# Half of the query projection moved into the pair products of a hybrid encoder layer

## The chip, the cores and the metric

The kernel runs on one core of one Trainium2 chip. The metric is device time in microseconds of one launch. Before the change it is 678.65 us, the median of three runs (678.29 to 679.68). The core has a matmul engine (TensorE, PE in the profile; its weight loads are PEld), a vector engine (VectorE, DVE), a scalar engine (ScalarE, ACT), a general engine (GpSimd, POOL) and a queue that issues the transfers (SyncE, SP). Each takes its own instructions strictly in order and waits for the others by semaphores.

## What is computed

One layer over 1024 tokens of width 1024, in float32: a layer norm, one input projection whose columns are cut into eight parts, two branches, and an output projection with a second layer norm.

```
proj = layer_norm(x) @ w_in                    # 1024 x 5120
q, k, v, z_a, u, z_b, g_a, g_b = split(proj)   # 4 x 512, 2 x 512, 2 x 1024
attn = neighbourhood_attention(q, k, v, rpb)   # 8 heads of 64, q scaled by 1/8
u = centred_depthwise_conv(u, conv_w, conv_b)
h = rg_lru(u, forward) + rg_lru(u, reverse)    # decay exp(-8 softplus(-lam) * gate)
m = sigmoid(g_a + b) * ((attn * silu(z_a)) @ w_ba) + sigmoid(g_b + b) * ((h * silu(z_b)) @ w_bb)
out = layer_norm(alpha * x + m @ w_out)
```

## The kernel before

**Numbers as high and low parts.** A matmul operand is kept as two tiles: a rounded "high" part (a cast, `..._hi`) and the "low" remainder (a subtraction, `lo_of`, line 128). A product of two such operands is three matmuls (`mm3`, line 134): high by high, high by low, low by high.

**First stage: layer norm, v and half of q.** The tokens are eight tiles of 128. `tile_in(i)` transposes tile i on TensorE into four blocks of the activation: B11, B21 hold the first four tiles, B12, B22 the last four; the first index is the half of the 1024 features. `v_part` and `q_part` multiply those blocks with weights directly. q is 512 columns, in four blocks m of 128; each `q_part(m, n)` with n for the half of the tokens is 24 matmuls of 512 columns. Before, all four m are made in this way: m = 0, 1 for the first tokens between the v parts, and six parts, (0, 1), (1, 1), (2, 0), (2, 1), (3, 0), (3, 1), behind the last v part. Each part is emptied by ScalarE (`q_hi`, scaled by 1/8) and VectorE (`q_lo`) and stored to `q_d`.

**The pairs.** The rest of `w_in`, except v, is done in pairs of 128-column blocks: 16 pairs. Each pair is a 2 x 2 block product in Winograd's form, with 7 block products in place of 8, in the order `OPS` = a11, a12, s2, s1, s3, s4, a22. A product is one slot, 4 x 3 = 12 matmuls of 512 columns. The loop over `7 * N_PAIR + 4` slots (line 1003) is the backbone of the middle of the kernel. The weights' side needs sums s1 to s4 of the pair's four blocks (`s_sum`, VectorE) and each operand's high (`s_hi`, ScalarE, or GpSimd for those in `HI_POOL` from pair 1 on) and low (`s_lo`, VectorE, or GpSimd for a11 and a22). The activations' side needs B11, B21, B22 and four sums T1 to T4, made once per tile 4 to 7:

- `t_full(i)`: t1, t2, t3 of the tile, one copy on ScalarE and four steps on VectorE;
- `t_last(i)`: t4 from t2 and B21, two steps on VectorE (lines 309 and 310);
- `t_hi`, `t_lo`: high on ScalarE, low on GpSimd.

Only a22, the last product of a pair, uses T4. The products s2, s3 and a22 add into the PSUM bank of a11 and s4 into that of s1. Between two of them `evacuate` copies the bank out on ScalarE (tiles u1 to u3, lines 939 to 945) or adds it on VectorE, so the next product into the bank waits for that.

**What a pair's result becomes** is set by the list `takes`: `take_u` for the convolution input, `take_zg` for gates, `take_k` for keys. A consumer may return two later steps, run one and two slots after.

**Slots.** Convolution, gates of the recurrence and the loads for the next stages are put at fixed slots (`CONV_AT`, `GATE_AT`, `LATE_AT`, `HEAD_AT`). Weights of pair p + 2 are loaded in the fifth slot of pair p (`s_load`). Pairs listed in `U_PAIRS` take no extra PSUM bank.

**The change of stage.** Behind the last q part the first stage's pools are released and PSUM is split anew into six banks for the pairs and two for the gates. There the decay rates of the recurrence (softplus of lam by a series, lines 626 to 642: one ScalarE exponential and some thirty tiny VectorE steps) are worked out, all in one block ahead of pair 0's VectorE work.

The order on ScalarE, VectorE, GpSimd and the SP queue is the order in which the code is written; TensorE's too. Attention, the branch projections, the merge and the output projection follow the pairs and aren't touched.

Of the kernel before, what the change touches and what calls it, by code (L numbers as in the profile page):

```python
# [10 lines left out]
F32 = mybir.dt.float32  # L11
# [28 lines left out]
BLOCKS = (1, 0, 6, 2, 3, 4, 5, 7)  # L40
# [27 lines left out]
def encoder_kernel(ctx, tc, x, gb1, gb, w_qk, w_v, w_s, w_ba, w_bb, w_gate, smalls, bias, w_out, out):  # L68
# [58 lines left out]
    def lo_of(eng, lo, full, hi):  # L127
        eng.tensor_tensor(lo, full, hi.bitcast(F32), ALU.subtract)  # L128
# [160 lines left out]
    def f(t, i):  # L289
        return t[:, :, ti(i)].bitcast(F32)  # L290

    def t_full(i):

        tt[i, 3] = wsp.tile([P, 4, P], F32, tag="a22", bufs=2, name=f"t3_{i}")[:]
        t12 = ln.tile([P, 2, 4, P], F32, tag="x", bufs=5, name=f"t12_{i}")
        tt[i, 1], tt[i, 2] = t12[:, 0], t12[:, 1]
        if i in (4, 6):
            tt["last"] = ln.tile([P, 2, 4, P], F32, tag="x", bufs=5, name=f"t4_{i}")
        tt[i, 4] = tt["last"][:, i % 2]
        t1, t2, t3 = (tt[i, c] for c in (1, 2, 3))  # L300
        A.copy(t3, tp4(i, 0))
        V.tensor_tensor(t1, tp4(i, 0), f(B11[0], i), ALU.subtract)
        V.tensor_tensor(t1, t1, f(B11[1], i), ALU.subtract)
        V.tensor_tensor(t2, tp4(i, 1), t1, ALU.subtract)
        V.tensor_tensor(t3, tp4(i, 1), t3, ALU.subtract)

    def t_last(i):
        t4 = tt[i, 4]
        V.tensor_tensor(t4, f(B21[0], i), tt[i, 2], ALU.subtract)
        V.tensor_tensor(t4, t4, f(B21[1], i), ALU.add)  # L310

    def t_hi(i, *cs):
        for c in cs:
            A.copy(Ts[c][0][:, :, ti(i)], tt[i, c])
# [54 lines left out]
    def s_load(p, *names):  # L369
        for o in names if p < N_PAIR else ():  # L370
            t = wsp.tile([P, 4, P], F32, tag=o, bufs=2 if o == "a22" else 1, name=f"{o}_{p}f")
            SP.dma_start(t[:], w_s[p, ("a11", "a21", "a12", "a22").index(o)])
            s_a[p, o] = t

    def s_sum(p, *names):
        for o in names if p < N_PAIR else ():
            a, b, op = dict(s1=("a21", "a22", ALU.add), s2=("s1", "a11", ALU.subtract),
                            s3=("a11", "a21", ALU.subtract), s4=("a12", "s2", ALU.subtract))[o]
            t = s_a[p, o] = wsp.tile([P, 4, P], F32, tag=o, name=f"{o}_{p}f")
            V.tensor_tensor(t[:], s_a[p, a][:], s_a[p, b][:], op)  # L380

    def s_hi(p, o):
        if p < N_PAIR:
            s_w[p, o] = pair(wsp, [P, 4, P], f"w{o}_{p}", tag="w" + o)
            (G.tensor_copy if p and o in HI_POOL else A.copy)(s_w[p, o][0][:], s_a[p, o][:])
# [157 lines left out]
    q_part(0, 0, slice(256, HALF))  # L543
    t_last(4)
    tile_in(5)
    q_hi(0, 0)
    t_hi(4, 2, 1, 3, 4)
    t_lo(4, 2, 1, 3, 4)
    tile_lo(5)
    q_lo(0, 0)  # L550
    q_store(0, 0)
    keep(7)
    q_part(1, 0)
    t_full(5)
    q_hi(1, 0)
    q_lo(1, 0)
    q_store(1, 0)
    t_last(5)
    for kind in "hwa":
        v_part(4, kind, KS)  # L560
    tile_in(6)
    v_hi(4)
    t_hi(5, 2, 1, 3, 4)
    t_lo(5, 2, 1, 3, 4)
    tile_lo(6)
    v_lo(4)
    v_store(4)
    t_full(6)
    for kind in "hwa":
        v_part(5, kind, KS)  # L570
    tile_in(7)
    v_hi(5)
    t_hi(6, 2, 1, 3)
    t_lo(6, 2, 1, 3)
    tile_lo(7)
    v_lo(5)
    v_store(5)
    t_last(6)
    t_hi(6, 4)
    t_lo(6, 4)  # L580
# [12 lines left out]
    s_load(0, "a11")  # L593
    for m in range(4):
        for n in BOTH if m > 1 else (1,):
            q_part(m, n)
            if m < 2:
                qk_prep(m + 2)
                if m == 0:
                    qk_load(3)  # L600
                    t_hi(7, 2, 1, 3, 4)
                    t_lo(7, 2, 1, 3, 4)
                    s_load(0, "a21", "a22", "a12")
                else:
                    s_sum(0, "s1", "s2", "s3", "s4")
            q_hi(m, n)
            q_lo(m, n)
            q_store(m, n)
            if m > 1:
                for w in (OPS[:2], OPS[2:4], OPS[4:6], OPS[6:])[2 * (m - 2) + n]:  # L610
                    s_hi(0, w)
                    s_lo(0, w)
    s_load(1, "a11", "a21", "a12", "a22")
    for pl in (ln, wpl, hb12, pst, ps0):
# [10 lines left out]
    lam = sm[:, SM_LAM:SM_LAM + 8]  # L625
    V.tensor_scalar(smh[:], sm[:], 0.5, None, ALU.mult)
    V.tensor_scalar(t0[:], lam, -1.0, None, ALU.mult)
    V.tensor_tensor(t0[:], lam, t0[:], ALU.min)
    A.activation(t0[:], t0[:], AF.Exp)
    V.tensor_scalar(t1[:], t0[:], 2.0, None, ALU.add)  # L630
    V.reciprocal(t1[:], t1[:])
    V.tensor_tensor(t0[:], t0[:], t1[:], ALU.mult)
    V.tensor_tensor(t1[:], t0[:], t0[:], ALU.mult)
    V.tensor_scalar(t2[:], t1[:], 1.0 / 21.0, 1.0 / 19.0, ALU.mult, ALU.add)
    for n in (17, 15, 13, 11, 9, 7, 5, 3, 1):
        V.tensor_tensor(t2[:], t2[:], t1[:], ALU.mult)
        V.tensor_scalar(t2[:], t2[:], 1.0 / n, None, ALU.add)
# [4 lines left out]
    V.tensor_scalar(nsp[:], t0[:], -C_LRU, None, ALU.mult)

# [827 lines left out]
```

## Time and profile before

| what | us |
|---|---|
| median of three runs | 678.65 |
| the profiled execution | 678.46 |
| its span, first to last instruction | 676.7 |
| TensorE busy | 665.2 (98%) |
| VectorE busy | 492.7 (73%) |
| ScalarE busy | 364.5 (54%) |
| GpSimd busy | 355.8 (53%) |

The granted TensorE clock was 0.997 on average. In time, the v parts end near 73 us, the six q parts stand from there to 105.6, the sixteen pairs run to about 426, attention to about 542 and the output to the end.

How the rows read: a row of the timeline gives start, length, engine, line, operation, the tile written and those read, the form and a count; in brackets the idle time before it and what ended it. A row of the chain of waits gives start, length and the work. A row of the waits gives who waited for whom, total, times and longest. "L128" is `lo_of` and "L134" `mm3`, whoever calls them, so the tile names say which step it is. In tile names numbers are left out: `a_0f` is any raw block of pair 0, `s_0f` any sum of it, `wa_h` and `ws_l` its high and low parts, `ht` the T blocks, `t` their full sums.

### The profile page before, as it was taken

The page shows a single profiled execution, that of the slowest core. Times are in us where ns is not written, and L with a number is a line of the kernel's source. Part 1 is how long each engine was busy: PE and PEld are TensorE (multiplying, and loading weights), DVE is VectorE, ACT ScalarE, POOL GpSimd, SP SyncE. Part 2 cuts the span into 40 slices and gives each one's busy share as a digit, 9 for nine tenths or more (in the row PEclk, how much of TensorE's full clock was granted, in tenths as well). Part 3 has the DMA queues.
Part 4 walks back from the last instruction along what each step waited for, and adds up shares of the span by engine and source line. Part 5 has one row for each costly group of instructions (what it writes and reads, how often), then busy time and mean ns, then how long its engine had stood idle before and what let it go on. Part 6 is the DMA issues. An engine that isn't in the chain of part 4 may idle for free.

```text
span 676.7 us, 9344 instructions
## 1 busy us (share of the span) xinstructions
PE 665.2 (98%) x3201; PEld 555.7 (82%) x3201; DVE 492.7 (73%) x821; ACT 364.5 (54%) x612; POOL 355.8 (53%) x258
## 2 busy tenths in 40 slices
PE   8999999999999999999999999999999999999995
PEld 6888888888888887888788888888888878888884
DVE  6978747886998699879967785477787787443434
ACT  6554433256786676669576634477777554210110
POOL 6798632434677576567647444116155456334442
PEclk9999999999999999999999999999999999999998
DMA  8654353233434133431553456998793467412211
GB/s 326 244 179 170 122 206 126 77 110 123 125 128 144 40 103 115 170 126 48 195 178 122 173 191 254 316 366 296 255 323 132 162 220 281 178 62 94 93 63 62
DMA packets 48702, 113.39 MB, mean 168 GB/s; under 512 B 5056, under 2 KB 9744, under 8 KB 47120
## 3 DMA queue, kind: packets, MB, share of 16 engines
q1 hardware_dynamic: 48624, 112.81, 47.2%
q8 instruction: 25, 0.41, 0.3%
q14 instruction: 21, 0.17, 0.1%
q10 hardware_dynamic: 32, 0.01, 0.0%
HBM read 77.11 MB, written 35.68 MB: 167 GB/s over the span
## 4 chain that ended last, share of the span: by engine, by line
PE 89%; DVE 6%; DMA 2%; issue 1%; SPq 1%; ACT 0%; POOL 0%; DVEq 0%; POOLq 0%
PE a L134 30%; PE o L134 13%; PE mb L134 12%; PE s L134 11%; PE q L134 6%; PE v L328 6%; PE acc L1107 3%; PE s L1061 3%; PE pt L1083 3%; PE g L759 2%; DMA wqk_s<-in_w_qk_dram 2%; DVE ws_l L128 1%; PE tp L270 1%; DMA rsb<-rs_d 1%; DVE uc L717 1%
## 5 line engine op out<-in xcount | busy, mean ns | idle before, releaser
L134 PE MATMUL o<-wo_h,ml 128*128 128x512 f32 (+1 forms) x136 | 51.2, 377 | 0.0
L134 PE MATMUL o<-wo_l,mh 128*128 128x512 f32 (+1 forms) x136 | 51.2, 376 | 0.0
L134 PE MATMUL o<-wo_h,mh 128*128 128x512 f32 (+1 forms) x136 | 51.2, 376 | 0.0
L134 PE MATMUL a<-ht_h,ws_h 128*128 128x512 f32 x128 | 50.0, 390 | 0.0
L134 PE MATMUL a<-ht_l,ws_h 128*128 128x512 f32 x128 | 49.8, 389 | 0.0
L134 PE MATMUL a<-ht_h,ws_l 128*128 128x512 f32 x128 | 49.8, 389 | 0.0
L134 PE MATMUL a<-b_h,wa_h 128*128 128x512 f32 x128 | 49.8, 389 | 0.0
L134 PE MATMUL a<-b_h,wa_l 128*128 128x512 f32 x128 | 49.8, 389 | 0.0
L134 PE MATMUL a<-b_l,wa_h 128*128 128x512 f32 x128 | 49.8, 389 | 0.0
L1071 DVE CUSTOM_DVE_ANT_0 sc<-s,bias 128x384 f32<-128x384 f32 (+1 forms) x64 | 33.4, 522 | 21.6 <-PE s L1061 14.2
L1361 DVE SCALAR_TENSOR_TENSOR z<-z,o 128x512 f32<-128x512 f32 (+1 forms) x17 | 11.2, 656 | 51.0 <-PE o L134 51.0
L1091 ACT CAST pt_h<-pt 128x384 fp32r<-128x384 f32 x64 | 29.0, 453 | 25.3 <-PE pt L1083 17.3
L1371 POOL TENSOR_TENSOR z<-z,gb 128x1024 f32<-128x1024 f32 x7 | 16.8, 2400 | 48.5 <-ACT z L1370 48.5
L1076 ACT ACTIVATE p<-sc,summ 128x384 f32<-128x384 f32 (+1 forms) x64 | 37.8, 591 | 5.5 <-DVE summ L1071 5.3
L1340 ACT ACTIVATE sd<-mv,eps_z 128x1 f32<-128x1 f32 x8 | 2.4, 294 | 67.1 <-DVE mv L1366 67.1
L128 DVE TENSOR_TENSOR pt_l<-pt,pt_h 128x384 fp32r<-128x384 f32 x64 | 33.2, 519 | 2.1 <-ACT pt_h L1091 1.6
L328 PE MATMUL v<-wv,b_h 128*128 128x512 f32 x128 | 32.9, 398 | 0.6 <-ACT b_h L279 0.5
L867 POOL CAST wb_h<-wb 128x512 fp32r<-128x512 f32 x9 | 7.0, 779 | 47.4 <-DMA wb<-in_w_bb_dram 47.4
L1061 PE MATMUL s<-ks,qs 128*128 128x384 f32 (+1 forms) x128 | 31.4, 327 | 0.0
L1083 PEld LDWEIGHTS pt<-ident,p 128*128 128x128 f32 x176 | 23.1, 140 | 8.5
L1083 PE MATMUL pt<-ident,p 128*128 128x128 f32 x176 | 29.6, 272 | 0.0
L128 POOL TENSOR_TENSOR wb_l<-wb,wb_h 128x512 fp32r<-128x512 f32 x16 | 22.0, 1375 | 14.3 <-ACT wb_h L865 13.6
(438 smaller groups left out, 2204.2 us busy)
## 6 DMA issues: line engine op xcount, KB each, us to landing
ks<-k_d SPq DMA_DIRECT2D x8, 1024.0 KB, 7.5
h_d<-x SPq DMA_DIRECT2D x8, 512.0 KB, 5.0
v_d<-vs SPq DMA_DIRECT2D x8, 512.0 KB, 3.7
q_d<-q SPq DMA_DIRECT2D x8, 512.0 KB, 3.1
ga_d<-ga SPq DMA_DIRECT2D x16, 256.0 KB, 2.2
gb_d<-gb SPq DMA_DIRECT2D x16, 256.0 KB, 2.6
k_d<-k SPq DMA_DIRECT2D x8, 512.0 KB, 3.4
qs<-q_d SPq DMA_DIRECT2D x8, 512.0 KB, 5.5
```

What stands on the lines that cost most here:

```text
L128: eng.tensor_tensor(lo, full, hi.bitcast(F32), ALU.subtract)
L134: PE.matmul(o, a, b, start=first and i == 0, stop=last and i == len(prods) - 1, skip_group_check=not (first and last))
L328: PE.matmul(vos[i][:], a, wv[kind == "w"][k][:], start=vn[i] == 0, stop=vn[i] == 23)
L759: PE.matmul(o[:, n, :], w[:, 2 * d + b, :], us[b][:, n * HALF:(n + 1) * HALF], start=z == 0, stop=z == 1)
L1061: PE.matmul(o[:, :P * len(near(t))], q[:, t * P:(t + 1) * P], k[:, z, keys], start=z == 0, stop=z == 1)
L1071: V.tensor_tensor_reduce(s[:, :w], o[:, :w], heads[h][2][:, b0:b0 + w], -1.0, 3.0e38, ALU.add, ALU.min, accum_out=sums[h][0][:, t:t + 1])
L1076: A.activation(probs[h % 2][t][:], scs.pop((h, t))[:, :w], AF.Exp, bias=sums[h][0][:, t:t + 1], scale=-1.0, accum_out=sums[h][1][:, t:t + 1])
L1083: PE.transpose(tp[:, n * P:(n + 1) * P], probs[h % 2][t][:, z * P:(z + 1) * P], ident[:])
L1091: A.copy(pt[0][:, span(b)], tps[h, b][:, :P * len(near(b))])
L1107: PE.matmul(acc[g][:, d:d + w], vvs[h // 2][:, b, h % 2, :], pt[:, a:a + w], start=b in (1, 6) and z == 0, stop=z == 1 and b == (4, 7)[g])
L1361: V.scalar_tensor_tensor(z[:, cols], z[:, cols], ALPHA * TWICE, o, ALU.mult, ALU.add)
L1371: G.tensor_tensor(z[:], z[:], gb2[:, 0, :], ALU.mult)
```

## The change

- q's blocks m = 2 and 3 become a new pair 0 (`N_PAIR` 17, first entry 2 in `heads`); the old pairs follow as 1 to 16, and all slot constants move by 7. A new consumer, `take_q`, scales the results by 1/8, splits them and stores them to `q_d`. Of the direct q parts four remain, two of them, (0, 1) and (1, 1), behind the last v part.
- `t_last` of all four tiles moves behind q's last part. t4 takes t2's place, so the tiles for t4 go. The lows of t4 are taken in the order of tiles 7, 4, 5, 6. The full t3 of tiles 5 and 6 lie in other buffers (`a21`, `a12`).
- `t_full(5)` moves ahead of `q_part(1, 0)`, and `t_hi` and `t_lo` stand right behind each `t_full`.
- Pair 0's raw blocks are loaded into other buffers (`ws`, `x`) behind `t_full(6)` and `t_full(7)`; its sums, highs and lows stand between the last v part and the last q part, all highs on ScalarE, all lows on VectorE. Pair 1's blocks are loaded one after the other from `t_full(7)` on.
- The decay rates become a generator, of which one piece is run in each of slots 8 to 13, in pair 1.

```diff
-N_PAIR = 16
+N_PAIR = 17
-CONV_AT = (7, 24, 45, 66)
-GATE_AT = (14, 24, 35, 45, 56, 66, 77, 87)
-LATE_AT = (102, 102, 103, 104, 105)
-HEAD_AT = 109
+CONV_AT = (14, 31, 52, 73)
+GATE_AT = (21, 31, 42, 52, 63, 73, 84, 94)
+LATE_AT = (109, 109, 110, 111, 112)
+HEAD_AT = 116
-U_PAIRS = (0, 5)
+U_PAIRS = (1, 6)
...
-        tt[i, 3] = wsp.tile([P, 4, P], F32, tag="a22", bufs=2, name=f"t3_{i}")[:]
+        tag = ("a22", "a21", "a12", "a22")[i - 4]
+        tt[i, 3] = wsp.tile([P, 4, P], F32, tag=tag, bufs=2 if tag == "a22" else 1, name=f"t3_{i}")[:]
...
     def t_last(i):
-        t4 = tt[i, 4]
-        V.tensor_tensor(t4, f(B21[0], i), tt[i, 2], ALU.subtract)
+        t4 = tt[i, 4] = tt[i, 2]
+        V.tensor_tensor(t4, f(B21[0], i), t4, ALU.subtract)
...
-            lo_of(G if o in LO_POOL else V, lo[:], s_a[p, o][:], hi[:])
+            lo_of(G if p and o in LO_POOL else V, lo[:], s_a[p, o], hi[:])
...
     for kind in "hwa":
         v_part(5, kind, KS)
+    s_load(0, "a11", "a12")
     tile_in(7)
...
     t_full(7)
+    t_hi(7, 2, 1, 3)
+    t_lo(7, 2, 1, 3)
+    s_load(0, "a21", "a22")
+    s_load(1, "a21")
     for kind in "hwa":
         v_part(6, kind, KS)
     v_hi(6)
-    t_last(7)
     v_lo(6)
     v_store(6)
+    s_load(1, "a12")
+    s_sum(0, "s1", "s2", "s3", "s4")
     for kind in "hwa":
         v_part(7, kind, KS)
     v_hi(7)
     v_lo(7)
     v_store(7)
-    s_load(0, "a11")
-    for m in range(4):
-        for n in BOTH if m > 1 else (1,):
-            q_part(m, n)
...
-    s_load(1, "a11", "a21", "a12", "a22")
+    s_load(1, "a11")
+    for o in OPS[:3]:
+        s_hi(0, o)
+        s_lo(0, o)
+    q_part(0, 1)
+    for o in OPS[3:5]:
+        s_hi(0, o)
+        s_lo(0, o)
+    q_hi(0, 1)
+    q_lo(0, 1)
+    q_store(0, 1)
+    s_load(1, "a22")
+    q_part(1, 1)
+    for o in OPS[5:]:
+        s_hi(0, o)
+        s_lo(0, o)
+    t_last(4)
+    q_hi(1, 1)
+    t_hi(4, 4)
+    t_last(5)
+    q_lo(1, 1)
+    q_store(1, 1)
+    for i in (5, 6, 7):
+        if i > 5:
+            t_last(i)
+        t_hi(i, 4)
+    for i in (7, 4, 5, 6):
+        t_lo(i, 4)
...
+    def take_q():
+
+        def consume(mi, n, add, o, c=None):
+            c = o if c is None else c
+            if add is not None:
+                V.tensor_tensor(c[:], add[:], o[:], ALU.add)
+            t = lru.tile([P, 2, HALF], F32R, tag=("us0", "r", "i", "us1")[2 * mi + n], name=f"q2{mi}{n}")
+
+            def high():
+                A.activation(t[:, 0, :], c[:], AF.Copy, scale=0.125)
+
+            def store():
+                V.scalar_tensor_tensor(t[:, 1, :], c[:], 0.125, t[:, 0, :].bitcast(F32), ALU.mult, ALU.subtract)
+                SP.dma_start(q_d[2 + mi][:, :, halves[n]], t[:].bitcast(F32))
+            return [high, store]
+        return consume
...
+    rates = decay_rates()
+    for slot in range(8, 14):
+        at(slot, 1, lambda: next(rates))
...
-    heads = [16, 20, 12, 24, 26, 18, 32, 22, 28, 34, 4, 30, 6, 14, 36, 38]
+    heads = [2, 16, 20, 12, 24, 26, 18, 32, 22, 28, 34, 4, 30, 6, 14, 36, 38]
```

More of the change, by code (lines that the diff above doesn't have):

```diff
@@ L369, in s_load @@
     def s_load(p, *names):
-        for o in names if p < N_PAIR else ():
-            t = wsp.tile([P, 4, P], F32, tag=o, bufs=2 if o == "a22" else 1, name=f"{o}_{p}f")
-            SP.dma_start(t[:], w_s[p, ("a11", "a21", "a12", "a22").index(o)])
+        for z, o in enumerate(names if p < N_PAIR else ()):
+            if p:
+                t = wsp.tile([P, 4, P], F32, tag=o, bufs=2 if o == "a22" else 1, name=f"{o}_{p}f")[:]
+            else:
+                if z == 0:
+                    place = dict(pool=ln, tag="x", bufs=5) if o == "a21" else dict(pool=wpl, tag="ws", bufs=1)
+                    both = place.pop("pool").tile([P, 2, 4, P], F32, name=f"{o}_{p}f", **place)
+                t = both[:, z]
+            SP.dma_start(t, w_s[p, ("a11", "a21", "a12", "a22").index(o)])
             s_a[p, o] = t
@@ L384, in s_hi @@
             s_w[p, o] = pair(wsp, [P, 4, P], f"w{o}_{p}", tag="w" + o)
-            (G.tensor_copy if p and o in HI_POOL else A.copy)(s_w[p, o][0][:], s_a[p, o][:])
+            (G.tensor_copy if p and o in HI_POOL else A.copy)(s_w[p, o][0][:], s_a[p, o])
     def s_lo(p, o):
@@ L543, in encoder_kernel @@
     q_part(0, 0, slice(256, HALF))
-    t_last(4)
     tile_in(5)
     q_hi(0, 0)
-    t_hi(4, 2, 1, 3, 4)
-    t_lo(4, 2, 1, 3, 4)
+    t_hi(4, 2, 1, 3)
+    t_lo(4, 2, 1, 3)
     tile_lo(5)
@@ L552, in encoder_kernel @@
     keep(7)
+    t_full(5)
     q_part(1, 0)
-    t_full(5)
     q_hi(1, 0)
@@ L557, in encoder_kernel @@
     q_store(1, 0)
-    t_last(5)
+    t_hi(5, 2, 1, 3)
+    t_lo(5, 2, 1, 3)
     for kind in "hwa":
@@ L568, in encoder_kernel @@
     t_full(6)
+    t_hi(6, 2, 1, 3)
+    t_lo(6, 2, 1, 3)
     for kind in "hwa":
         v_part(5, kind, KS)
+    s_load(0, "a11", "a12")
     tile_in(7)
     v_hi(5)
-    t_hi(6, 2, 1, 3)
-    t_lo(6, 2, 1, 3)
     tile_lo(7)
```

71 lines of the change are left out of this document (26 added, 45 removed).

## The prediction

> **What bounds the kernel now.** I read the page's first part, then the chain of waits, then what TensorE waited for.
>
> ```profile
> span 676.7 us, 9344 instructions
> PE 665.2 (98%) x3201; PEld 555.7 (82%) x3201; DVE 492.7 (73%) x821; ACT 364.5 (54%) x612; POOL 355.8 (53%) x258
> ```
>
> ```profile
> 62.03 10.90 PE v L328 x48
> 72.93 32.64 PE q L134 x144
> 105.57 8.16 PE a L134 x36
> 113.73 2.72 PE s L134 x12
> ```
>
> ```profile
> PE v L328 <- ACT b_h L279: 0.5, 1, 0.5
> PE a L134 <- DVE w L792: 0.4, 1, 0.4
> ```
>
> PE is busy 98% of the span, and the chain (start, length, engine and tile) runs on PE without a break from v through q into the products of pair 0. The longest waits behind the first microseconds are 0.5 and 0.4 us. So matmuls taken away come off the end, as long as nothing makes PE wait. The price of a matmul is its spacing in the chain: 32.64 / 144 = 0.2267 us, or 2.72 us for the 12 of a product. The page's mean of 389 ns counts overlap.
>
> **The change: what goes off PE.** The six q parts in that chain row cost 32.64 / 6 = 5.44 us each. Four of them (m = 2, 3) go: -21.76. A pair comes: 7 x 2.72 = +19.04. Net -2.72 us. Nothing else that PE issues changes in number; the slot numbers of convolution, gates and late stages all move by 7, one pair. The question is whether the other engines still keep up, since pair 0 now starts at 72.93 + 10.88 = 83.81 instead of 105.57, 21.76 us sooner, and its weights and T blocks must be ready by then.
>
> **Stage before 73 us (v).** The block sums of tiles 4 to 6 now do without `t_last` on DVE, ACT and POOL:
>
> ```profile
> 50.70 1.12 DVE L309 TENSOR_TENSOR t<-b_h,t 128x512 f32<-128x512 f32 x1
> 51.86 1.66 DVE L310 TENSOR_TENSOR t<-t,b_l 128x512 f32<-128x512 f32 x1
> 74.89 0.69 DVE L302 TENSOR_TENSOR t<-tp,b_h 128x512 f32<-128x512 f32 x1 [1.17 <-ACT t L301]
> 77.54 0.68 DVE L309 TENSOR_TENSOR t<-b_h,t 128x512 f32<-128x512 f32 x1
> 78.26 0.69 DVE L310 TENSOR_TENSOR t<-t,b_l 128x512 f32<-128x512 f32 x1
> 78.87 1.28 DVE L128 TENSOR_TENSOR vs<-v,vs 128x512 fp32r<-128x512 f32 x2
> 52.93 5.50 POOL L128 TENSOR_TENSOR ht_l<-t,ht_h 128x512 fp32r<-128x512 f32 x4
> 81.91 5.02 POOL L128 TENSOR_TENSOR ht_l<-t,ht_h 128x512 fp32r<-128x512 f32 x4
> ```
>
> A `t_last` is 2.78 us while POOL works (first two rows) and 1.33 while it is idle (77.54 to 78.87). Three leave this stretch, so DVE, which before reached the v lows of tiles 6 and 7 at 78.87, reaches tile 6's by about 70. Tile 7's transposes end at 62.03, unmoved. Behind them come, at 0.54 us a cast (2.17 / 4, below), three `t_hi(6)` and two `turn_hi` on ACT (to about 64.7), then on DVE `tile_lo(7)`, `v_lo(5)` and four operations of `t_full(7)` (seven at 0.6 to 0.7, to about 69), and three lows on POOL (1.3 each, from about 69 to 73). PE loses its cover nowhere here; its inputs come sooner. The dropped `qk_load`, `qk_hi`, `qk_lo` of m = 2, 3 free ACT and POOL; I count them as nothing, being off PE's chain already.
>
> **The tail, 73 to 89 us.** This is where DVE's own queue decides. Ahead of it stand the sums, which wait for pair 0's loads; the loads now stand behind `v_store(5)` on SP, which `v_lo(5)` releases at about 66, so I take 66.9 for the last of the two that the first sum needs.
>
> ```profile
> DMA to landing us min/median/max: 4.9/5.3/5.8
> 89.28 1.85 DVE L380 TENSOR_TENSOR s_0f<-a_0f 128x512 f32<-128x512 f32 x1 [5.33 <-DMA a_0f<-in_w_s_dram]
> 91.17 0.69 DVE L380 TENSOR_TENSOR s_0f<-s_0f,a_0f 128x512 f32<-128x512 f32 x1
> 94.18 0.68 DVE L128 TENSOR_TENSOR wa_l<-a_0f,wa_h 128x512 fp32r<-128x512 f32 x1
> 106.23 0.69 DVE L360 SCALAR_TENSOR_TENSOR q<-q,q 128x512 fp32r<-128x512 f32 x1 [3.55 <-ACT q L355]
> 105.60 0.60 ACT L355 ACTIVATE q<-q 128x512 fp32r<-128x512 f32 x1 [3.82 <-PE q L134]
> 79.37 2.17 ACT L314 CAST ht_h<-t 128x512 fp32r<-128x512 f32 x4
> 108.55 0.57 ACT L939 COPY u<-a 128x512 f32<-128x512 f32 x1
> ```
>
> The first row is the landing of pair 0's loads. With its median the sums start at 72.2. In order, at 0.61 us a step (0.72 where one needs the one before): four sums to 74.8, `v_lo(7)` to 75.4, five lows to 78.4. `q(0,1)` ends on PE at 78.37, its high on ACT at 79.2, its low at 79.8; two lows to 81.0; `t_last(4)` and `(5)` to 83.7. `q(1,1)` ends at 83.81, its high at 84.4 (ACT starts 0.03 behind, as at 105.60 against 105.57 in the chain), its low at 85.1. So DVE is 0.7 us ahead there, and 0.8 more lies in its gap at 78.4. `t_last(6)` and `(7)`, 1.33 + 1.37, end at 87.8 and the high of T4's tile 7 at 88.4. Behind that on ACT stands the copy of pair 0's first sum, to 89.0. The product s2 adds into the same bank and waits for that copy; it is due at 83.81 + 5.44 = 89.25. Slack 0.25 us over eight steps in a row, each of which may be some hundredths longer: bounds 0 and 0.4, and I put 0.1 us of stall.
>
> This holds because POOL does nothing meanwhile: `t_lo(7, 4)` is its first item and waits for that same high. With tiles 4 to 6 first, the last two `t_last` would cost 2.78 each and s2 would come about 2 us late. So that order is worth about 2 us only as a cost avoided.
>
> **Pair 0, 89 to 103 us.** POOL starts T4's four lows at 88.5 and needs 5.02 to 5.50: 93.5 to 94.0. T4 is used at 100.1, so that is hidden. But pair 1's high parts queue behind it on POOL, and DVE's lows behind those.
>
> ```profile
> 113.41 0.62 POOL L385 CAST wa_h<-a_1f 128x512 fp32r<-128x512 f32 x1 [5.34 <-DVE sp L637]
> 113.99 1.29 POOL L128 TENSOR_TENSOR wa_l<-a_1f,wa_h 128x512 fp32r<-128x512 f32 x1
> 118.16 1.09 DVE L128 TENSOR_TENSOR wa_l<-a_1f,wa_h 128x512 fp32r<-128x512 f32 x1
> 119.17 0.68 DVE L380 TENSOR_TENSOR s_1f<-a_1f,s_1f 128x512 f32<-128x512 f32 x1
> 119.78 1.09 DVE L128 TENSOR_TENSOR ws_l<-s_1f,ws_h 128x512 fp32r<-128x512 f32 x1
> 120.79 0.68 DVE L658 TENSOR_TENSOR up<-u,a 128x512 f32<-128x512 f32 x1
> ```
>
> After the cast of a12 (0.62, to 94.7 at the latest) DVE does low a12, sum s4, low s2 (when cast), a store of q and the add that empties the a11 bank; product a22 waits for that add and is due at 83.81 + 6 x 2.72 = 100.13. By these rows: 94.7 + 1.09 + 0.68 + 1.09 + 0.6 + 0.68 = 98.8. With all three as slow as the 1.66 row it is 101.0. The bounds of the stall are 0 and 0.8; I take 0.1, near the rows of this very place. Before, the same add ended at 121.47, 0.4 us ahead of its product (105.57 + 16.32 = 121.89).
>
> The Trainium skill ("SBUF — State Buffer", "Who interferes with whom") has a rule that speaks against the change: a VectorE instruction with two SBUF inputs and a GpSimd one that reads SBUF exclude each other for a whole instruction. The trace agrees so far: 1.66 and 1.85 us against 0.68, never more than one POOL operation (1.29) on top. By that rule each of the three steps would wait out one POOL instruction, which is the first rival below.
>
> **Pair 1, 103 to 122 us.** The rates, a block of DVE work ahead of pair 0's before, are now cut into slots 8 to 13.
>
> ```profile
> 106.84 1.28 DVE L626 TENSOR_SCALAR smh<-sm 128x60 f32<-128x60 f32 x1
> 108.04 0.16 DVE L627 TENSOR_SCALAR sp<-sm 128x8 f32<-128x8 f32 x1
> 115.42 0.17 DVE L642 TENSOR_SCALAR nsp<-sp 128x8 f32<-128x8 f32 x1
> 112.98 0.17 DVE L636 TENSOR_TENSOR sp<-sp,sp 128x8 f32<-128x8 f32 x1
> 105.50:124.50 19.00, 19.00 (x86) 15.73 (x85) 16.41 (x48) 4.88 (x8) 6.50 (x7) 1.00 0.48 152
> 130.76 1.82 DVE L380 TENSOR_TENSOR s_2f<-a_2f 128x512 f32<-128x512 f32 x1
> 133.70 1.09 DVE L128 TENSOR_TENSOR wa_l<-a_2f,wa_h 128x512 fp32r<-128x512 f32 x1
> 134.72 1.78 DVE L380 TENSOR_TENSOR s_2f<-a_2f,s_2f 128x512 f32<-128x512 f32 x1
> 107.96 2.05 SPq L372 DMA_DIRECT2D a_1f<-in_w_s_dram  x4
> a_1f<-in_w_s_dram SPq DMA_DIRECT2D x4, 256.0 KB, 3.9
> ```
>
> They take 115.6 - 106.8 = 8.8 us, the same work as before in the pair with the same other work (DVE 16.41 of 19.00 us, rates in it), plus three leftover q steps (0.6 each, 1.9 with their waits): 18.3 of 19.04. Tight, not over. The point of decision is the add ahead of a22 of pair 1, due at 102.85 + 16.32 = 119.2. DVE starts when pair 2's loads land; on SP they stand behind q's first store (98.2), at 2.05 / 4 = 0.51 an issue the last goes out at 100.3 and lands 3.9 later, 104.2. Then six two-input steps (four at 0.69, two at 1.09: 4.9), the q steps 1.9, an add 0.7, 20 of the rates' steps (1.28, and 19 at (112.98 - 108.04) / 23 = 0.21: 5.3), the add 0.7: 117.7. Slack 1.5, so no stall. From pair 2 on, slots and work are those of before.
>
> **Sum.** Profiled execution 678.46 (span 676.7 and 1.8 around it) - 2.72 + 0.1 + 0.1 = 675.9. The median of the three runs, 678.65, lies 0.19 above the profiled one, so 676.1 us.
>
> **Rivals.** *DVE and POOL exclude each other in pair 0.* Low a12, s4 and low s2 all cost 1.66: a22 waits 0.8 instead of 0.1, 676.8. For it: 1.66, and 1.85 at 89.28. Against: 0.68 at 119.17 in the same place. By the Trainium skill's rule above, with the POOL instructions that stand there (1.29, 0.62, 0.62 on top of 0.68), a22 would wait 0.4, which is 676.4.
>
> *DVE overfull in pair 1.* With the six steps as the next pair had them (1.82, 1.78, 1.09 and three at 0.69: 6.8) the add ends at 119.6, 0.4 late. With loads that land in 5.8, as some of pair 0's did, 1.9 more. That gives 676.5 to 678.4, middle 677.4, about the bound of no change. For it: 18.3 of 19.04. Against: POOL is busy for only 6.50 us in that stage.
>
> *The other side: every such step of DVE in pair 1 contended.* If the spread rates put all six beside POOL's work, 6 x 1.8 = 10.8 instead of 4.9, the add ends at 123.6, 4.4 late: 680.5. It makes the kernel slower than now from 9.1 us for the six (4.9 + 1.5 slack + 2.7 saved), measurably from 10.5. For it: 1.82 and 1.78 in a pair with less small work on DVE, and then pair 2 starts with DVE behind. Against: before, with the rates in one block, the same six met two contentions.
>
> *The loads come too late.* If pair 0's blocks land over 6.8 us after issue, the 0.7 + 0.8 of the tail is gone (72.2 + 1.5), and PE waits one for one at s2. These loads' rows (at most 5.8) are against it. At 9 us: 2.2, 678.3.
>
> *The change takes nothing off PE.* Excluded by 144 matmuls in 32.64 us without a gap.
>
> **How the numbers follow.** About 0.2% (1.36 us) is what a measurement of this kernel can tell from no change; faster thus means under 677.3, slower over 680.0. Forecast, with stalls up to 0.6: 0.48. Exclusion in pair 0 (676.8): 0.17, faster too. DVE overfull: 0.18, half of it under 677.3. Late loads: 0.05, same. All contended: 0.12, slower. Faster 0.48 + 0.17 + 0.09 = 0.74; same 0.14; slower 0.12. The range starts at 675.4 (no stall, 675.9, less the 0.4 by which the lowest run lies under the median, and a little) and ends at 678.4, the end of the overfull case, which leaves out the slower one. The forecast's own range is 675.6 to 676.7.
>
> **What would show it.** In the chain after: q x48 for 10.88 us behind v, then a x24 at about 83.8, each product 2.72. PE waits named by u (the copy L939) under 0.3 us, and none by x's adds. If DVE is overfull, a PE wait on a DVE add appears at about 119; if loads are late, DVE's idle time before s_0f names a DMA and the first copy of u comes after 89.3. T4's lows should start near 88.6 with DVE's last two `t_last` at 0.69 each. It would be wrong if PE shows a gap of over 1.4 us anywhere between 84 and 125.

## The result and the profile after

The changed kernel takes 675.61 us, the median of six runs (674.93 to 676.07), against 678.50 for the kernel before on the same chip: 0.9955 of it, with a 95% interval of 0.9942 to 0.9968. So it is faster by 0.32 to 0.58%, where 0.2% can be told from no change. The profiled execution took 676.07 us against 678.46. Of the executions of the experiments below, one with the rates in one block and one with `t_last` early took about 3000 us and are left out of the comparisons. From the first part of the page after:

```profile
span 674.3 us, 9352 instructions
PE 663.7 (98%) x3189; PEld 554.3 (82%) x3189; DVE 498.9 (74%) x835; ACT 364.5 (54%) x615; POOL 354.4 (53%) x261
```

PE is still the bound. To see where the 2.4 us of the span come from, both traces are cut at the same places of the program, not at the same times. The first cut is the start of the last v matmul: ahead of it the start of the kernel varies by 1.6 us from one execution to the next (71.8 to 73.4 us over all profiles but those of the experiments e3b and e10, which change what stands ahead of the cut). This arises in the first 30 us, and kernels with and without the change overlap there; the two profiles here differ by 0.06.

| stretch on PE | before | after | difference |
|---|---|---|---|
| last v matmul to the first product of the pairs | 32.87 | 11.11 | -21.76 |
| from there to the first product of the merge (the pairs) | 320.75 | 340.95 | +20.20 |
| to the first transpose of attention's probabilities | 11.91 | 11.95 | +0.04 |
| to the last product of attention with v | 98.34 | 98.31 | -0.03 |
| to the last product of the merge | 44.59 | 43.47 | -1.12 |
| to the end | 95.69 | 95.91 | +0.22 |
| sum | 604.13 | 601.69 | -2.44 |

The forecast was -21.76, and +19.04 plus 0.2 of stalls for the pairs, and nothing elsewhere. So the pairs cost 0.96 us more than forecast and the merge 1.12 us less: the stretches that the change touches gained 1.56 us, where 2.52 was forecast, and the merge made up for the rest. The timeline of PE after shows the places that the prediction named (start, length, engine, line, operation, tiles):

```profile
83.71 0.39 PE L134 MATMUL a<-b_h,wa_h 128*128 128x512 f32 x1
...
88.92 0.39 PE L134 MATMUL a<-b_l,wa_h 128*128 128x512 f32 x1
89.15 0.42 PE L134 MATMUL a<-ht_h,ws_h 128*128 128x512 f32 x1
...
99.85 0.39 PE L134 MATMUL s<-b_l,ws_h 128*128 128x512 f32 x1
100.19 0.50 PE L134 MATMUL a<-ht_h,wa_h 128*128 128x512 f32 x1
...
119.17 0.39 PE L134 MATMUL s<-b_l,ws_h 128*128 128x512 f32 x1
119.63 0.50 PE L134 MATMUL a<-ht_h,wa_h 128*128 128x512 f32 x1
```

Two products of 12 matmuls lie between 83.71 and 89.15, 5.44 us: no gap ahead of s2. Ahead of a22 the step from start to start is 0.34 in pair 0 and 0.46 in pair 1, instead of 0.2267; with the slower matmul behind each gap the losses are 0.23 and 0.33 us. The gates of the recurrence, which lie among the pairs, give the next piece. In the rows of the tile g (how long one matmul takes in ns, least, median and most), before, after, and in one experiment:

```profile
L759 PE MATMUL g<-us,gw_h x32: 389/389/389, 146.2 to 365.9; 128*128 128x512 f32 x32
```

```profile
L794 PE MATMUL g<-us,gw_h x32: 394/394/394, 144.2 to 364.3; 128*128 128x512 f32 x32
```

```profile
L795 PE MATMUL g<-us,gw_h x32: 395/396/398, 144.7 to 364.7; 128*128 128x512 f32 x32
L795 PE MATMUL g<-us,gw_l x32: 387/390/397, 144.9 to 364.9; 128*128 128x512 f32 x32
```

By the median all 64 take 5 ns longer after, though their program text did not change, and within a group of four the step from one start to the next is 233.3 ns instead of 226.7. With the two steps behind each group this comes to 0.45 us. Stalls 0.56 and gates 0.45 make 1.01 of the 1.16 us by which the pairs exceed 19.04; the other 0.15 is spread over single steps.

### The profile page after: what moved, and what is told of

The parts are those of the page before. It is cut to its first block, busy times and chain, and to the rows that moved or that the text cites. A ratio compares the mean times of both kernels' runs of the same rounds, so it can differ in the third digit from the quotient of the medians.

```text
span 674.3 us, 9352 instructions
## 1 busy us (share of the span) xinstructions
PE 663.7 (98%) x3189; PEld 554.3 (82%) x3189; DVE 498.9 (74%) x835; ACT 364.5 (54%) x615; POOL 354.4 (53%) x261
## 4 chain that ended last, share of the span: by engine, by line
PE 76%; DVE 9%; issue 4%; POOL 1%; ACT 1%; DMA 1%; SPq 0%; DVEq 0%; POOLq 0%
PE a L134 28%; PE o L134 13%; PE mb L134 13%; PE s L134 11%; PE acc L1145 4%; PE s L1099 3%; PE pt L1121 3%; PE g L794 2%; POOL ht_l L128 1%; DVE ws_l L128 1%; DVE wa_l L128 1%; DMA a_2f<-in_w_s_dram 1%; DVE uc L752 1%; ACT ht_h L312 1%; DVE s_12f L384 0%
## 5 line engine op out<-in xcount | busy, mean ns | idle before, releaser
L134 PE MATMUL a<-ht_h,ws_h 128*128 128x512 f32 x136 | 53.1, 391 | 0.0
L134 PE MATMUL a<-ht_h,ws_l 128*128 128x512 f32 x136 | 53.0, 389 | 0.0
L134 PE MATMUL a<-b_h,wa_l 128*128 128x512 f32 x136 | 53.0, 389 | 0.0
L134 PE MATMUL a<-ht_l,ws_h 128*128 128x512 f32 x136 | 52.9, 389 | 0.0
L134 PE MATMUL a<-b_h,wa_h 128*128 128x512 f32 x136 | 52.9, 389 | 0.0
L134 PE MATMUL a<-b_l,wa_h 128*128 128x512 f32 x136 | 52.9, 389 | 0.0
L128 POOL TENSOR_TENSOR ht_l<-t,ht_h 128x512 fp32r<-128x512 f32 x16 | 22.0, 1408 | 19.9 <-ACT ht_h L312 19.9
L134 PEld LDWEIGHTS a<-ht_h,ws_h 128*128 128x128 f32 x136 | 25.5, 188 | 5.9 <-issue 0.4
```

What stands on the lines that cost most here:

```text
L134: PE.matmul(o, a, b, start=first and i == 0, stop=last and i == len(prods) - 1, skip_group_check=not (first and last))
```

## Experiments

Each has a short name (e0 to e10), which the table at the end uses.

**Is the gain in the merge chance?** (e0) The kernel before once more, unchanged.

> The kernel before, profiled a second time. In the first profile TensorE loses 1.0 us more in attention and the start of the merge (427 to 545 us) than the changed kernel does. If that is chance of a run (transfers of the softmax sums), this profile shows a smaller loss there and the products' part unchanged; if it belongs to the kernel, the same loss comes again.

678.75 us; behind the last v matmul 604.13 again, and in the merge 44.56 against 44.59. So the 1.12 us belongs to the kernels, not to the execution.

**The order of T4's lows** (e1).

```diff
-    for i in (7, 4, 5, 6):
+    for i in (4, 5, 6, 7):
         t_lo(i, 4)
```

> Only the order of T4's lows on GpSimd: tiles 4, 5, 6, 7 in place of 7, 4, 5, 6. Theory (the last two block sums on VectorE must run beside an idle GpSimd): they cost 2.8 us each in place of 1.35, the copy of pair 0's first sum comes 2 to 2.5 us later, TensorE waits that long ahead of s2, 677.6 to 678.1 us. Rival (the tail has slack, the order is of no weight): 675.6, no wait ahead of s2.

679.44 us (1.0009 of before, 0.9998 to 1.002): the whole gain is gone, 3.8 us against the changed kernel by the medians. Behind the last v matmul the profile has 604.68 us against 601.69, 3.0 more. PE's timeline, and below it the stretch from 92 to 96 us (busy time of the engines, then the granted clock):

```profile
89.58 0.39 PE L134 MATMUL a<-b_l,wa_h 128*128 128x512 f32 x1
91.81 0.50 PE L134 MATMUL a<-ht_h,ws_h 128*128 128x512 f32 x1 [1.84 <-ACT u L977]
...
93.12 0.63 PE L134 MATMUL a<-ht_h,ws_l 128*128 128x512 f32 x1
```

```profile
92.00:96.00 4.00, 4.00 (x11) 3.15 (x11) 3.96 (x4) 0.28 (x1) 3.70 (x3) 0.57 0.02 4
```

The wait is the forecast one: s2 waits for the copy of u, which stands behind the high of T4's tile 7 on ACT, and that behind `t_last`, which POOL's lows now hold up. It takes 91.81 - 89.58 - 0.23 = 2.0 us. What nobody forecast comes behind it: matmuls of 627 ns, 0.43 us apart, with a granted clock of 0.57 in that stretch. From 92.38 to 96.02 nine steps take 3.64 us instead of 2.04, 1.6 us on top of the wait. Both stalls ahead of a22, 0.56 us, are gone in turn. The twelve times reach from 677.84 to 682.64 us and one was profiled, so how often the slow matmuls come isn't known.

**The rates in one block** (e2).

```diff
-    rates = decay_rates()
-    for slot in range(8, 14):
-        at(slot, 1, lambda: next(rates))
+    for _ in decay_rates():
+        pass
```

> The decay rates in one block ahead of pair 0's work, as before the change, all else as changed. Theory (VectorE's and ScalarE's queues decide the start of the pairs): the exponential and its table load stand ahead of the copy that s2 waits for, 1 to 1.5 us of stall there, and VectorE comes to the add ahead of a22 of pair 0 some 3 us late; the stall of 0.3 at a22 of pair 1 goes. 678.5 to 680. Rival (the rates are small and hidden wherever they stand): 675.3 to 675.8.

685.72 us (1.0101, 1.0086 to 1.0116), 10 us more than the changed kernel and some 6 more than the higher forecast. The timeline of DVE, ACT and PE:

```profile
88.39 0.18 DVE L639 TENSOR_SCALAR smh<-sm 128x60 f32<-128x60 f32 x1
94.17 0.55 DVE L640 TENSOR_SCALAR sp<-sm 128x8 f32<-128x8 f32 x1 [5.59 <-POOL ht_l L128]
...
96.42 0.57 ACT L976 COPY u<-a 128x512 f32<-128x512 f32 x1
...
97.05 0.80 PE L134 MATMUL a<-ht_h,ws_h 128*128 128x512 f32 x1 [7.14 <-ACT u L976]
```

It isn't the length of the block that costs most. The rates' first small tile `sp` waits 5.59 us for POOL's lows of T4, the last of which reads a tile in whose place `sp` now stands (in the program as built, the tile with t4 of tile 6 takes bytes 163552 to 167648 of a partition, `sp` 163648 to 163680); the exponential on ACT waits for `sp`, and the copy of u stands behind the exponential. PE waits 7.1 us, and the ten steps behind that take 4.43 us instead of 2.27, with a granted clock of 0.50 from 97 to 101 us. A block of DVE work had become a wait for POOL by a reused buffer. The slots avoid it, since POOL has long finished by slot 8.

**T4's last steps between the v parts again** (e3, and e3b for its profile). The `t_last`, high and low of tiles 4, 5 and 6 stand behind `t_lo` of tiles 5, 6 and 7, and tile 7's ahead of `q_hi(1, 1)`.

```diff
     t_hi(5, 2, 1, 3)
     t_lo(5, 2, 1, 3)
+    t_last(4)
+    t_hi(4, 4)
+    t_lo(4, 4)
...
     for o in OPS[5:]:
         s_hi(0, o)
         s_lo(0, o)
-    t_last(4)
+    t_last(7)
+    t_hi(7, 4)
+    t_lo(7, 4)
     q_hi(1, 1)
```

> The block sums t4 of tiles 4 to 6 go back between the v parts, each one tile later than its other sums, that of tile 7 stands ahead of q's last low. Theory (VectorE beside GpSimd has no room for them in the v stage): they cost 2.8 us each there, ScalarE's highs of tile 7 come behind them, TensorE waits 0.5 to 1.2 us ahead of the v part of tile 7, and wins back 0.2 at a22 of pair 0, whose GpSimd queue is then free: 676.0 to 676.8. Rival (the place of t4 is of no weight): 675.4 to 675.6, no wait in the v stage.

> The same kernel as the one with the last parts of T4 of tiles 4 to 6 ahead of the sums, for a profile of it. It took 1.9 us more than the changed kernel. If the v stage is what pays, v low of tile 6 or the four sums end later than 70 and 74.8 us and PE shows gaps before pair 0; if pair 0 pays, the copy of u ahead of s2, or the low of s2 and the add ahead of a22, end after 89.3 and 100.1 us. Expected: sums end about 2.7 us later (two t_last, 1.37 us each, between the v parts), the lows of the eight operands of pair 0 with them, and a gap of about 1.9 us at the start of pair 0 or in it.

677.54 us, the median of eleven runs (0.9983 of before, 0.9974 to 0.9992), 677.56 in the execution that was profiled: 1.9 us more than the changed kernel. ACT's row ahead of the longest wait and PE's timeline:

```profile
67.79 0.62 ACT L312 CAST ht_h<-t 128x512 fp32r<-128x512 f32 x1 [1.23 <-DVE t L308]
66.62 1.52 PE L326 MATMUL v<-wv,b_l 128*128 128x512 f32 x6
68.95 0.72 PE L326 MATMUL v<-wv,b_h 128*128 128x512 f32 x2 [0.81 <-ACT b_h L279]
```

PE now loses 1.1 us in v (the step from 67.75 to 68.95 and the slower one behind it), as the first forecast had it. The parts of tile 7 wait for ACT's casts of its transposes; these stand behind a high of T4 (67.79), and that waits for a `t_last` on DVE. Another 0.6 us goes ahead of pair 0, and the two stalls ahead of a22 are won back (0.56). That makes 1.1 us; the rest of the 1.9 isn't accounted for, and the start of the kernel alone varies by as much. The granted clock stays at 1.00 behind the step of 1.2 us. So `t_last` out of the v stage is worth 1 to 2 us, more in v than in the tail.

**The two stalls ahead of a22, each alone.** Two of T4's four lows on DVE (e5):

```diff
-    for i in (7, 4, 5, 6):
+    for i in (7, 4):
         t_lo(i, 4)
+    for i in (5, 6):
+        lo_of(V, Ts[4][1][:, :, ti(i)], tt[i, 4], Ts[4][0][:, :, ti(i)])
```

> Of T4's four lows those of tiles 5 and 6 go from GpSimd to VectorE, which in the changed kernel waits 4.2 us for GpSimd's first cast of pair 1. Theory (both remaining stalls, 0.2 us ahead of a22 of pair 0 and 0.3 ahead of a22 of pair 1, come from that late queue): GpSimd is free at about 91.5 in place of 94.5, both stalls go, 0.5 us less: 675.1. Rival (VectorE's two steps are contended and only move the lateness): both stalls stay, 675.6.

```profile
98.41 0.68 DVE L706 TENSOR_TENSOR c<-u,a 128x512 f32<-128x512 f32 x1
...
89.10 3.33 POOL L128 TENSOR_TENSOR ht_l<-t,ht_h 128x512 fp32r<-128x512 f32 x2 [15.53 <-ACT ht_h L312]
```

676.11 us (0.9960, 0.9948 to 0.9972). POOL is done with T4 at 92.43 instead of 94.54, the add ahead of a22 of pair 0 ends at 99.09, and that stall is gone. Pair 1's is gone too in this execution, as q's first store and the loads behind it come a microsecond sooner.

Two of pair 2's four loads ahead of q's first store (e6):

```diff
-            s_load(p + 2, "a11", "a21", "a12", "a22")
+            s_load(p + 2, *(("a11", "a12") if p == 0 else ("a11", "a21", "a12", "a22")))
+        if slot == 3:
+            s_load(2, "a21", "a22")
```

> Two of pair 2's four blocks (a21, a22) are loaded one slot sooner, ahead of q's first store on the SP queue. Theory (the stall ahead of a22 of pair 1 comes from these loads: VectorE waits 4.8 us for them): the wait shrinks to under 2.5 us and the 0.3 us of stall goes, the stall ahead of a22 of pair 0 stays: 675.3. Rival (VectorE is overfull in pair 1 whatever the loads do): the stall stays.

```profile
116.68 0.69 DVE L676 TENSOR_TENSOR up<-u,a 128x512 f32<-128x512 f32 x1
...
90.70 1.03 SPq L376 DMA_DIRECT2D a_2f<-in_w_s_dram  x2
```

675.66 us (0.9957, 0.9945 to 0.9969). The loads go out at 90.70, and the add ahead of a22 of pair 1 ends at 117.4: that stall is gone, pair 0's (0.25) stays, as it should. The total of neither differs from the changed kernel's beyond the intervals.

**Where the gates' input lies** (e4). In the program as built, the tile `us` lies at 184288 bytes of a partition before and at 163744 after, 96 and 32 bytes above a multiple of 128. Two of the rates' small tiles are allotted later, which brings it to 163680, again 96 above one.

```diff
-    t0, t1, t2 = (lru.tile([P, 8], F32, name=f"sp{c}") for c in range(3))
+    t0 = lru.tile([P, 8], F32, name="sp0")
...
         A.activation(t0[:], t0[:], AF.Exp)
         yield
+        t1, t2 = (lru.tile([P, 8], F32, name=f"sp{c}") for c in (1, 2))
```

> Two tiny tiles of the decay rates (32 bytes a partition each) are allotted later, so the tiles that the gate matmuls read (us) lie 64 bytes lower; no instruction changes. In the changed kernel all 64 gate matmuls follow each other at 233 ns, before at 227. Theory (the place of the tile in SBUF sets this): 227 ns again, 0.4 us less. Rival (the pitch hangs on something else, such as what runs beside): 233 ns, no gain.

676.18 us (0.9966, 0.9954 to 0.9978). The pitch changed, from an even 233.3 ns to steps between 224 and 238 with a mean of 232.0, but didn't come back to 226.7 (the last of the three fences on g above). The gates' weights, which had moved too between before and after, lie in e4 where they lie after. So moving `us` alone changes the pitch, and the place within 128 bytes is not the rule. Which rule it is stays open.

**The three together** (e7).

> The three edits together: us tiles 64 bytes lower, two of T4's lows on VectorE, pair 2's a21 and a22 loaded sooner. Theory: both stalls of 0.2 and 0.3 us and the 0.4 us of the gate matmuls go, 674.7. Rival: under 0.3 us less than the changed kernel.

675.72 us (0.9962, 0.9950 to 0.9974). Behind the last v matmul it takes 600.79 us against 601.69, with both stalls gone, but its time can't be told from that of the changed kernel: 0.9 us is within what the start varies.

**The round trip in front of the merge.** The last head's sums `rs` are stored to DRAM and read back spread over 64 rows (`rsb`); POOL multiplies `za` with them, and the merge's last operand waits for that. The queue's and POOL's rows, before and after, and the instructions that DMA fetched within 2 us of the store's issue:

```profile
531.06 0.28 SPq L1131 DMA_DIRECT2D rs_d<-rs  x1
532.66 0.45 SPq L1138 DMA_DIRECT2D rsb<-rs_d  x1
...
537.04 2.54 POOL L1145 TENSOR_TENSOR za<-za,rsb 128x512 f32<-128x512 f32 x2 [9.54 <-DMA rsb<-rs_d]
```

```profile
q14 instruction: 1, 0.01, 1.1%
q1 hardware_dynamic: 16, 0.00, 1.0%
```

```profile
529.56 0.28 SPq L1169 DMA_DIRECT2D rs_d<-rs  x1
530.79 0.45 SPq L1176 DMA_DIRECT2D rsb<-rs_d  x1
...
534.43 2.56 POOL L1183 TENSOR_TENSOR za<-za,rsb 128x512 f32<-128x512 f32 x2 [8.40 <-DMA rsb<-rs_d]
```

```profile
q1 hardware_dynamic: 16, 0.00, 1.0%
```

The trip is 5.98 us before and 4.87 after. Its first part, from issue to issue, is 1.60 against 1.23. Three kernels tried what makes it so. The first (e8) gives the kernel before the longer array of weights.

```diff
-    heads = [16, 20, 12, 24, 26, 18, 32, 22, 28, 34, 4, 30, 6, 14, 36, 38]
+    heads = [16, 20, 12, 24, 26, 18, 32, 22, 28, 34, 4, 30, 6, 14, 36, 38, 2]
```

> The kernel before, unchanged in its instructions, but given the array of weights of the changed kernel: seventeen pairs, of which the last is never read. In both profiles of the kernel before, 5.98 and 5.95 us pass from the issue of the last head's store of rs to the start of POOL's za (the round trip through DRAM), and PE loses 3.17 and 3.15 us between 427 and 545 us. In the seven profiles of kernels with the change the trip is 4.70 to 5.27 us and the loss 2.16 to 2.35. Theory A, that the place of the arrays in DRAM sets the trip: with the longer array the trip falls to 5.3 us or less, the loss to about 2.2, and the kernel before gains about 1.0 us (677.5). Theory B, that what went ahead in the program sets it (the number of transfers, the time at which it comes): trip 5.9 to 6.0, loss 3.2, time 678.5. The rates of the gates' matmuls stay at 226.7 ns in either case, since no tile in SBUF moves.

678.77 us (1.0003, 0.9993 to 1.0012), trip 6.17. The length of the array isn't it. The second (e9) issues two transfers more.

```diff
         SP.dma_start(rs_d[h], r[:])
+        if h == 0:
+            for _ in range(2):
+                SP.dma_start(rs_d[h], r[:])
```

> The kernel before with the first head's store of rs issued three times instead of once, so that as many transfers have gone ahead of the last head's round trip as in the changed kernel, which issues two more than the kernel before (523 against 521). The two more cost SP about 2 x 0.3 us at a place with 4 us of slack. Theory B (the transfers that went ahead): the last trip falls from 5.95 to 5.98 us to 5.3 or less, and PE's loss between 427 and 545 us from 3.2 to about 2.2; 677.5 us. Theory A (the place in DRAM) and a rival of both (the time at which the trip falls, or the tiles' places in the stages ahead): trip 5.9 to 6.0, loss 3.2, time 678.5.

679.15 us (1.0010, 0.9997 to 1.0024), trip 5.82. Their number isn't it either. In both, as in every kernel with a slow first part, a piece of program is fetched close to the store. The third (e10) shifts the places of these fetches.

```diff
     V.memset(zero[:], 0.0)
     clock = bank("clock")
+    for _ in range(10):
+        V.memset(eps_z[:], EPS * TWICE * TWICE)
+        A.activation(warm[:], eps_t[:], AF.Sqrt)
+        G.memset(gb_t[1][1][:, 0:1], 0.0)
+    for _ in range(16):
+        PE.matmul(clock[:, 0:1], zero[:], zero[:, 0:1], start=True, stop=True)
```

> The kernel before with idle instructions at its start: ten small memsets each on VectorE and POOL, ten small square roots on ACT, sixteen matmuls of one column on PE, all dropped or overwritten. They only shift each engine's instructions against the places at which more of the program is fetched. In all four profiles with the instructions of the kernel before, queue q14 moves 8 KB of instructions 0.44 to 0.71 us after the issue of the last store of rs, and q8 16 KB at 2.33 to 3.04 us; the store's part of the round trip is 1.60 to 1.87 us, the trip 5.82 to 6.17. In the changed kernel they lie at -2.37 and +6.16, the store's part is 1.23, the trip 4.87. Theory C, that these fetches lie in the way: q8 is PE's (one per 107 to 150 matmuls), and sixteen matmuls bring it 16 x 0.2267 = 3.6 us earlier, to -1.3; q14's goes some us earlier if it is VectorE's, ACT's or POOL's, and stays if it is SP's. With both gone the store's part is 1.23 us, the trip 4.7 to 5.3, PE's loss between 427 and 545 us 2.2 instead of 3.2, and the time behind the last v matmul 603.2 instead of 604.13; with q14's still there the store's part stays 1.6. Theory D, that another thing moved by the change sets the trip: 5.8 to 6.2 us, loss 2.9 to 3.2, 604.1. The start costs up to 0.8 us more: 677.5 to 678.5 in all under C, 678.5 to 679.5 under D.

684.96 us (1.0089, 1.0072 to 1.0105). The total says nothing here: the ten square roots stand ahead of ACT's first load, `gb_row`, which goes out at 4.38 us instead of 0.73; PE waits 7.5 us for it, and the start takes 7.5 us longer. The trip is what counts. Over thirteen profiles (q14 and q8 are the queues that fetch program; fetches in us from the issue of the store, the merge as in the table above):

| kernel | first part | trip | fetch on q14 | fetch on q8 | merge |
|---|---|---|---|---|---|
| before | 1.60 | 5.98 | +0.44 | +2.33 | 44.59 |
| e0 | 1.60 | 5.95 | +0.45 | +2.38 | 44.56 |
| e8 | 1.66 | 6.17 | +0.45 | +3.04 | 44.79 |
| e9 | 1.87 | 5.82 | +0.71 | +2.45 | 44.45 |
| e10 | 1.76 | 5.71 | -2.59 | -0.31 | 44.34 |
| e2 | 1.73 | 5.21 | +0.36 | +5.04 | 43.81 |
| after | 1.23 | 4.87 | -2.37 | +6.16 | 43.47 |
| e1 | 1.23 | 4.74 | -2.41 | +5.32 | 43.47 |
| e3b | 1.23 | 4.78 | -2.40 | +5.79 | 43.51 |
| e4 | 1.23 | 4.74 | -2.37 | +5.96 | 43.45 |
| e5 | 1.23 | 5.27 | -2.41 | +6.02 | 43.91 |
| e6 | 1.23 | 4.99 | -2.43 | +5.59 | 43.61 |
| e7 | 1.23 | 4.70 | -2.43 | +5.09 | 43.45 |

Two things are plain. The merge takes 43.45 us plus what the trip has over 4.83, to 0.06 us in every row; where the trip is shorter than that, nothing is left to wait for. So the 1.12 us is the trip. And a first part of 1.60 or more goes with a fetch between 0.31 us ahead of the store and 0.71 behind it, in six of six; without one it is 1.23, in seven of seven. The shift of e10 moved q14's fetch out, as theory C had it, but q8's came to -0.31 instead of -1.3, next to the store, and the first part stayed long; the trip fell to 5.71, between the two theories, and the time behind the last v matmul was 604.08, as D had it. So the fetch is the only one of the suspects that goes with the first part, but no run showed it short in the kernel before. And the first part is only 0.37 of the 1.11 us by which the trip is shorter after. The second part (4.38 us before, 3.64 after) has no cause yet that separates the kernels: e5, e9 and e10, with 4.04, 3.95 and 3.95, lie between. So that the gain comes from this trip is shown; that a fetch close by lengthens its first part is likely, not shown; what shortens its second part, two thirds of the gain, stays open.

## Why the prediction was right, and where it was not

The forecast was 676.1 us, the measurement 675.6 (for the profiled execution 675.9 against 676.07), and the likeliest case, faster with small stalls, came. The path was right: PE is the bound, matmuls taken off it come off the end, and the other engines nearly keep up. That the total fits so well is luck, since a gain that no step had covers what the pairs lost. By its steps:

**What goes off PE** was exact: 21.76 us less ahead of the pairs, and a pair of 19.04 us where nothing stalls it (the new pair 0 took 19.37).

**The v stage** lost nothing, as said. What the prediction put down as inputs that "come sooner" was more: with `t_last` back there, PE waits (1.1 us there, in e3b).

**The tail** came as written. The rows after, DVE first, then ACT and POOL:

```profile
70.31 0.69 DVE L128 TENSOR_TENSOR vs<-v,vs 128x512 fp32r<-128x512 f32 x1 [1.61 <-ACT vs L333]
70.92 1.00 DVE L384 TENSOR_TENSOR s_0f<-a_0f 128x512 f32<-128x512 f32 x1
71.96 1.67 DVE L384 TENSOR_TENSOR s_0f<-s_0f,a_0f 128x512 f32<-128x512 f32 x1
...
79.15 0.69 DVE L358 SCALAR_TENSOR_TENSOR q<-q,q 128x512 fp32r<-128x512 f32 x1 [0.71 <-ACT q L353]
...
84.54 0.69 DVE L358 SCALAR_TENSOR_TENSOR q<-q,q 128x512 fp32r<-128x512 f32 x1 [0.84 <-ACT q L353]
...
87.19 0.69 DVE L308 TENSOR_TENSOR t<-t,b_l 128x512 f32<-128x512 f32 x1
...
87.91 0.62 ACT L312 CAST ht_h<-t 128x512 fp32r<-128x512 f32 x1 [0.71 <-DVE t L308]
88.44 0.58 ACT L977 COPY u<-a 128x512 f32<-128x512 f32 x1
...
68.83 4.24 POOL L128 TENSOR_TENSOR ht_l<-t,ht_h 128x512 fp32r<-128x512 f32 x3 [2.34 <-ACT ht_h L312]
```

The lows of q end at 79.84 and 85.23 (79.8 and 85.1 forecast), the last `t_last` at 87.88 (87.8), the copy of u at 89.02 (89.0). No stall followed; 0.1 was put. One agreement is luck: the sums began at 70.92, not at 72.2, since the loads had landed, but the first two met POOL's lows. The second ends at 73.63, 0.56 us behind POOL's 73.07. That is the exclusion of the Trainium skill ("SBUF — State Buffer", "Who interferes with whom"). Here the trace agrees with it: the contended steps of DVE between 70 and 99 us end 0.54 to 0.56 us behind the end of a POOL operation. So four sums end at 74.83 where 74.8 was forecast, by two errors of opposite sign.

**The order of the lows** did avoid a cost, and the wait was sized rightly, 2 us. The slow matmuls behind the wait, 1.6 us more, were not foreseen.

**Pair 0's stall**, bounded by 0 and 0.8 and taken as 0.1, was 0.23: a term of the sum mis-sized. The last piece of the chain of waits there (the landing of pair 2's last load), and the timeline of POOL, DVE and SP:

```profile
102.59 5.32 DMA a_2f<-in_w_s_dram
```

```profile
88.61 5.93 POOL L128 TENSOR_TENSOR ht_l<-t,ht_h 128x512 fp32r<-128x512 f32 x4 [15.54 <-ACT ht_h L312]
94.48 0.61 POOL L389 CAST wa_h<-a_1f 128x512 fp32r<-128x512 f32 x1
95.05 1.29 POOL L128 TENSOR_TENSOR wa_l<-a_1f,wa_h 128x512 fp32r<-128x512 f32 x1
...
95.13 1.77 DVE L128 TENSOR_TENSOR wa_l<-a_1f,wa_h 128x512 fp32r<-128x512 f32 x1 [4.22 <-POOL wa_h L389]
96.82 1.09 DVE L384 TENSOR_TENSOR s_1f<-a_1f,s_1f 128x512 f32<-128x512 f32 x1
97.84 1.09 DVE L128 TENSOR_TENSOR ws_l<-s_1f,ws_h 128x512 fp32r<-128x512 f32 x1
...
99.45 0.68 DVE L704 TENSOR_TENSOR c<-u,a 128x512 f32<-128x512 f32 x1
...
99.56 0.51 SPq L712 DMA_DIRECT2D q_d<-q  x1
100.21 2.71 SPq L376 DMA_DIRECT2D a_2f<-in_w_s_dram  x4
...
107.99 0.69 DVE L384 TENSOR_TENSOR s_2f<-a_2f 128x512 f32<-128x512 f32 x1 [4.82 <-DMA a_2f<-in_w_s_dram]
...
118.89 0.69 DVE L676 TENSOR_TENSOR up<-u,a 128x512 f32<-128x512 f32 x1
```

T4's lows took 5.93 us, not 5.02 to 5.50: the first two took 1.74 us each, while DVE did sums of pair 1, and the last two 1.29. So POOL pays in the exclusion as well, which the sum had counted only against DVE. Low a12, s4 and low s2 took 1.77, 1.09 and 1.09 instead of 1.09, 0.68 and 1.09. The low of a12 ends at 96.90, again 0.56 us behind a POOL operation, the one that ends at 96.34. The add came at 100.13, not at 98.8. The first rival, all three at 1.66, was half right; its 0.4 by the Trainium skill's rule lies about as far off as the 0.1. With two of the lows taken off POOL (e5) the stall was gone.

**Pair 1's stall**, put at none with 1.5 us of slack, was 0.33: the second mis-sized term. The rates fitted and DVE wasn't overfull: the six two-input steps took 4.6 us, where 4.9 was put, and one of them was contended (1.10), so that both rivals of pair 1 fall. The loads were late. q's first store went out at 99.56 instead of 98.2, the four issues took 2.71 instead of 2.05, and the last landed 5.3 us on instead of 3.9; DVE stood still for 4.82 us and its add ended at 119.58 instead of 117.7. With the loads sooner (e6) DVE starts 4.9 us sooner, counted from the start of pair 0, and the stall is gone. It belongs in part to the execution: in e4 the loads go out as late, DVE starts 0.9 us sooner, and there is no stall either. So e6, with one profile, bears the cause out without settling it.

**What no step had:** 1.12 us gained in the merge, 0.45 lost in the gates, 0.15 in the pairs and 0.22 in the output. They come to a gain of 0.3, which covers most of the 0.36 by which the stalls were sized too low. Without the merge the profiled span would have gained 1.3 us, about the 1.36 that the prediction could just tell from no change.

## What to carry to other kernels

Put the last operation of a chain that PE waits for ahead of everything that may contend with its predecessors, and look also for the reused buffer behind a wait: the order of four lows was worth 3 to 4 us, and one small tile in a reused place most of 10. When two engines exclude each other, add the time to both. And cut both traces at the same places of the program before a gain is credited to an edit; 1.1 of the 2.4 us gained in the span came from a stage whose text did not change.

## What was not expected of the hardware

- A wait of PE of 2.0 us (e1) was followed by nine steps between matmuls of 0.40 us on average instead of 0.23 (granted clock 0.57), 1.6 us more; a step of 1.2 us (e3b) by none. The Trainium skill ("TensorE: Matmul & The Clock Gate", "What's actually happening") has the clock fall after at least one idle window of about 3.4 us. Here, in one profile, it came behind a shorter gap, and the measurement decides.
- The spacing of the same matmuls was 226.7, 232.0 or 233.3 ns as their input tile lay elsewhere in SBUF (between the first and the other two their weights had moved too).
- The first part of a store and load through DRAM took 1.23 us, and 1.60 to 1.87 with a fetch of instructions close by (seen together in thirteen profiles, not shown as the cause).
